# One product of each channel unit in two column parts, in a two-layer hybrid decoder trunk in float32

## The chip, the core and the metric

The kernel runs on one core of one Trainium2 chip. The metric is the device time of one execution in microseconds; lower is better.

## What is computed

The reference is a decoder trunk of two layers on an input of 256 tokens with 1024 features, all in float32. A layer is a half-step SwiGLU feed-forward network (FFN), a mixing block with two branches (a Mamba-2 state-space branch and a gated DeltaNet branch) on the same normalised input, and a second FFN:

```python
for l in range(DEPTH):                                   # DEPTH = 2, D_FF = 2816
    h = h + 0.5 * swiglu(rms_norm(h, ffn1_norm[l]), ffn1_w_in[l], ffn1_w_out[l])
    u = rms_norm(h, mix_norm[l])
    (z_s, xbc, dt_s, qkv, z_d, b_d, a_d, gate_s, gate_d) = jnp.split(u @ w_in[l], split_points, axis=-1)
    y_s = mamba2_branch(z_s, xbc, dt_s, ...)
    y_d = deltanet_branch(qkv, z_d, b_d, a_d, ...)
    merged = sigmoid(gate_s) * (y_s @ ssm_w_branch[l]) + sigmoid(gate_d) * (y_d @ dn_w_branch[l])
    h = h + merged @ w_out[l]
    h = h + 0.5 * swiglu(rms_norm(h, ffn2_norm[l]), ffn2_w_in[l], ffn2_w_out[l])
return rms_norm(h, final_norm)
```

The change touches the products of the normalised input with the first FFN matrix (`ffn1_w_in`, `ffn2_w_in`: all but their first 256 gate and up columns) and with those parts of `w_in` whose channels are needed on partitions: q, k, v and the output gate of the DeltaNet branch, and x, B and C of the Mamba branch.

## The kernel before

**Three products for one.** TensorE works on float32r, a rounded float32. To keep float32 accuracy each operand is split into a high half (its value rounded to float32r) and a low half (the rest), and a product is made as high x high + high x low + low x high, accumulated in PSUM. Each line of the kernel that issues a matmul issues one weight load with it; the profile shows both, as PE and PEld.

**Weights.** All large weights are streamed once, in an order fixed beforehand, in pieces of 128 x 1024. `load` (line 147) brings a piece by DMA into a `wraw` buffer (five of them), and `prep` splits it: ScalarE writes `whi` (line 67), VectorE writes `wlo` (line 70), into five buffers each. `take` hands the next split piece to a user and issues loads and splits ahead of it.

**Channel units.** The normalised input stands transposed in one tile `uW`, as eight k tiles of 128 features; each k tile has 256 token columns of the high half (`uTh`) and 256 of the low half (`uTl`). `chan_chunk` makes one channel unit: 256 output channels, in two halves `a` of 128, for all 256 tokens. It takes two weight pieces; for each half and each of the eight k tiles `mm3w` issues three matmuls whose stationary operand is a 128 x 128 block of weights and whose moving operand is 256 token columns: line 301 (high x high), line 302 (high weights x low input), line 303 (low weights x high input). A unit is so 2 x 8 x 3 = 48 matmuls into one PSUM bank. In the profile a unit goes by the name of its bank: `fc` in the FFNs, and `kk`, `qq`, `vv`, `zd`, `bc`, `xs` in the mixing block.

Each FFN has 20 such units and each mixing block 28 (four each of k, q, v, the output gate and B/C, eight of x), which makes 2 x (2 x 20 + 28) = 136 in all.

**What stands around them.** In an FFN a first unit in token layout (tile `f`, matmuls of 512 columns, lines 296 to 298) comes before the `fc` units. The first pair of `fc` units is broken by four transposes (`gT`, line 498). After groups of four or two `fc` units come block products with 512 columns (tile `p`), and at the end the closing products (tile `o`). Behind a unit, ScalarE and VectorE apply SiLU and the gate (FFN) or a short convolution of four taps (mixing block). In the mixing block the order of the units and of the small matmuls between them (triangular inverse, recurrence, decays) is written out by hand in `ORDER`; a scheduler puts every engine's instructions in order from priorities.

**Small matmuls.** Some matmuls of the mixing block are in plain float32: `psp` (line 635, 16 moving columns), `lb` (line 694, 32 columns), `cbb` (line 973, 256 columns). The profile records a plain float32 product as two matmuls.

Of the kernel before, what the change touches and what calls it, by code (L numbers as in the profile page):

```python
# [30 lines left out]
NSPL = 5  # L31
START = 2
PLACES = 6 * [40]

# [16 lines left out]
def trunk_kernel(ctx, tc, x, wst, wsm, norms, lpar, rpar, cst, out):  # L53
    nc = tc.nc
    V, A, G, PE = nc.vector, nc.scalar, nc.gpsimd, nc.tensor
# [121 lines left out]
    def ahead(key, n, fn):  # L177
        while state[key] < n:
            fn(state[key])
            state[key] += 1  # L180

    def take():
        j = state["taken"]
        state["taken"] = j + 1
        ahead("loaded", min(plan[min(j + NSPL, n_forms) - 1][2] + NRAW - 1, n_raw), load)
        ahead("prepped", min(j + 1 if state["hold"] else j + NSPL, n_forms), prep)
        return halves.pop(j)
# [44 lines left out]
    uT = uTh = uTl = None  # L232
    places = list(PLACES)

# [62 lines left out]
        PE.matmul(ps, lh, rl, start=False, stop=False)  # L297
        return PE.matmul(ps, ll, rh, start=False, stop=stop)  # L298

    def mm3w(ps, wh, wl, mh, ml, start, stop):  # L300
        PE.matmul(ps, wh, mh, start=start, stop=False)  # L301
        PE.matmul(ps, wh, ml, start=False, stop=False)  # L302
        PE.matmul(ps, wl, mh, start=False, stop=stop)  # L303

    def tok_chunk(ps, ks):

        ws = [(k, take()) for k in ks[::2]]
        for t in range(2):
            for k0, (wh, wl) in ws:
                for k in range(2):  # L310
# [8 lines left out]
                        kt == KT - 1,  # L319
                    )  # L320

    def chan_chunk(ps):

        ws = [take(), take()]
        for a in range(2):
            for q in range(2):
                wh, wl = ws[q]
                for k in range(4):
                    kt = 4 * q + k
                    c0 = k * 256 + a * P  # L330
                    mm3w(
                        ps[:, a * 256 : (a + 1) * 256],
                        wh[:, c0 : c0 + P],
                        wl[:, c0 : c0 + P],
                        uTh[:, kt, :],
                        uTl[:, kt, :],
                        kt == 0,
                        kt == KT - 1,
                    )

    def out_chunks(ps, stat, ks, last, group=1, split=False, first=None):
# [87 lines left out]
    def ffn(nxt):  # L429
# [55 lines left out]
        for c in range(FC - 1):  # L485
            g2 = tmp2("g2")
            for a in range(2):
                ps = accb("fc")
                chan_chunk(ps)
                sg = s2.tile([P, S], F32, tag="ca", name="sg", bufs=2)  # L490
                act(sg[:], ps[:, 0:S], AF.Silu)
                tt(g2[:, a * S : (a + 1) * S], sg[:], ps[:, S : 2 * S], ALU.mult)
                todo = todo[1:]
                if c == 0 and a == 0:
                    bank = trb("gT")
                    for k in range(2):
                        for t in range(2):
                            PE.transpose(bank[:, k * S + t * P : k * S + (t + 1) * P], gt[t][:, k * P : (k + 1) * P], ident)
                    split(0, bank[:].rearrange("p (k t) -> p k t", k=2))
            split(2 * c + 2, g2[:].rearrange("p (k t) -> p k t", k=2))  # L500
            if c + 1 <= PAIRS[-1][-1]:
                block_sums(c + 1, g2)
            if todo[0] == "A":
                if not pb:
                    pb.update({i: trb(f"p{i}") for i in (1, 6, 5, 7)})
                four = [
                    (pb[1], lambda p: stat(2 * p, 0), PAIRS[n]),
                    (pb[5], lambda p: sums(p, 0), PAIRS[n]),
                    (pb[7], lambda p: sums(p, 2), PAIRS[n]),
                    (pb[6], lambda p: sums(p, 1), PAIRS[n]),  # L510
                ]
                block_products(four, n == 0, n == len(PAIRS) - 1)
                todo = todo[1:]
                n += 1
# [5 lines left out]
    def mixer(l, nxt):  # L520
# [202 lines left out]
        def k_unit(hp):  # L723
            ps = accb("kk")
            chan_chunk(ps)
            for a in range(2):
                conv(ps[:, a * S : (a + 1) * S], 2 * hp + a, kP[:, hp, :, a, :], False)

            def rest():
                ktb, nb = turned(kP, hp)  # L730
                ts(kq[:, hp], nb[:], EPS, ALU.add)
                c1 = small([P, 4], "c1")
                V.reciprocal(out=c1[:], in_=kq[:, hp])
                tt(c1[:], c1[:], Bp[:, hp], ALU.mult)
                stt(c3n[:, hp], c1[:], -1.0, eG[:, hp], ALU.mult, ALU.mult)
                kkb = trb("kkb")
                own(kkb, kP, kP, hp)
                kk = s2.tile([P, 4, 64], F32, tag="s2", name="kk")
                for c in range(4):
                    act(kk[:, c], kkb[:, c * 64 : (c + 1) * 64], scale=c1[:, c : c + 1])  # L740
                for a in range(2):
                    rows_ = slice(64 * a, 64 * a + 64)
                    qev["ins"] = tt(Q[rows_, 4 * hp : 4 * hp + 4, rows_], dN[rows_, 4 * hp : 4 * hp + 4], kk[rows_], ALU.mult)
                for c in range(3):
                    act(kd[:, c, hp, :], ktb[:, c * P : (c + 1) * P], scale=dT[:, 4 * hp + c, 63:64])
                rsqrt(c2[:, hp], kq[:, hp], [P, 4])
                G.tensor_tensor(out=c2[:, hp], in0=c2[:, hp], in1=Bp[:, hp], op=ALU.mult)
                yield

            return rest()  # L750

        def q_unit(hp):
            ps = accb("qq")
            chan_chunk(ps)
            for a in range(2):
                conv(ps[:, a * S : (a + 1) * S], 8 + 2 * hp + a, qP[:, hp, :, a, :], False)

            def rest():
                _, nb = turned(qP, hp)
                ts(oe[:, hp], nb[:], EPS, ALU.add, EPS * 128.0, ALU.mult)  # L760
                qkb = trb("qkb")
                own(qkb, kP, qP, hp)
                for a in range(2):
                    rows_ = slice(64 * a, 64 * a + 64)
                    qk = qkb[rows_, 0:256].rearrange("p (c i) -> p c i", c=4)
                    tt(AT[rows_, 4 * hp : 4 * hp + 4, rows_], dT[rows_, 4 * hp : 4 * hp + 4], qk, ALU.mult)
                yield

            return rest()
# [589 lines left out]
```

## Time and profile before

| what | value |
|---|---|
| median of three runs | 1572.18 us (1570.56 to 1574.96) |
| the profiled execution | 1574.73 us |
| its span (first to last instruction) | 1573.0 us |
| granted TensorE clock | 0.999 |
| matmuls and weight loads recorded | 11432 each |
| high x high products of `fc` (line 301) | 1280, mean 281 ns |
| splitting a weight piece on VectorE (`wlo`, line 70) | 1222 ns each |
| splitting a weight piece on ScalarE (`whi`, line 67) | 1060 ns each |

In the profile a matmul's duration runs from its start to the end of its results; the next one starts long before that, so what a stream of matmuls costs is the step from start to start. "Idle before" is the time an engine had nothing to do ahead of a group of instructions.

### The profile page before, as it was taken

Reading aid. Unit: us, or ns where it says so; the run is one execution under the profiler, and the core shown is the slowest. Engines: PE = TensorE matmul, PEld = TensorE weight load, DVE = VectorE, ACT = ScalarE, POOL = GpSimd, SP = SyncE. Lnnn points to the kernel's source line nnn. Section 1 sums busy time; section 2 is a strip of 40 time slices with the busy share of each in tenths; the row PEclk is TensorE's granted clock in tenths of the full one; section 3 lists DMA queues with packets and bytes.
Section 4 is the critical chain, followed back from the end, with each engine's and each line's share of the span. In section 5 each row is a group of like instructions: output and inputs, shape, how many; then the busy total and the mean of one; then the engine's idle time right before and its main releaser. Section 6 shows DMA issues by size and latency. Waiting matters only on the chain.

```text
span 1573.0 us, 28904 instructions
## 1 busy us (share of the span) xinstructions
PE 1544.0 (98%) x11432; PEld 1393.4 (89%) x11432; DVE 1254.2 (80%) x1888; ACT 950.7 (60%) x1534; POOL 53.8 (3%) x60
## 2 busy tenths in 40 slices
PE   8999999999999999999999999999999999999997
PEld 7999779999888888999789997899998888899995
DVE  6878868967899766878777888699589987677887
ACT  5656568766666645555555566776756665455554
POOL 0000010000000000000000001010000000000000
PEclk9999999999999999999999999999999999999999
DMA  8565565553565566565765456555345556555554
GB/s 297 199 201 186 185 213 188 168 164 114 180 212 164 183 205 192 169 207 181 243 206 191 166 186 223 192 188 188 115 137 200 175 185 215 176 191 187 161 186 133
DMA packets 94221, 293.12 MB, mean 186 GB/s; under 512 B 22325, under 2 KB 23301, under 8 KB 93062
## 3 DMA queue, kind: packets, MB, share of 16 engines
q1 hardware_dynamic: 94086, 291.29, 56.5%
q8 instruction: 89, 1.46, 0.4%
q14 instruction: 46, 0.38, 0.1%
HBM read 289.33 MB, written 1.92 MB: 185 GB/s over the span
## 4 chain that ended last, share of the span: by engine, by line
PE 68%; DVE 14%; DMA 7%; issue 5%; ACT 4%; POOL 1%; SPq 0%; POOLq 0%; ACTq 0%; DVEq 0%
PE fc L301 9%; PE fc L302 9%; PE fc L303 9%; DVE wlo L70 7%; DMA wraw<-in_wst_dram 4%; PE b L298 3%; PE t L297 3%; PE t L296 2%; PE t L298 2%; PE b L297 2%; PE b L296 2%; DVE ca L73 2%; ACT whi L67 2%; PE p L297 2%; PE p L298 2%
## 5 line engine op out<-in xcount | busy, mean ns | idle before, releaser
L70 DVE TENSOR_TENSOR wlo<-wraw,whi 128x1024 fp32r<-128x1024 f32 x488 | 592.3, 1222 | 176.8 <-ACT whi L67 172.3
L67 ACT ACTIVATE whi<-wraw 128x1024 fp32r<-128x1024 f32 x488 | 511.9, 1060 | 276.9 <-PE fc L302 96.0
L301 PE MATMUL fc<-uW,whi 128*128 128x256 f32 x1280 | 359.2, 281 | 0.0
L303 PE MATMUL fc<-uW,wlo 128*128 128x256 f32 x1280 | 358.9, 280 | 0.0
L302 PE MATMUL fc<-uW,whi 128*128 128x256 f32 x1280 | 358.9, 280 | 0.0
L303 PEld LDWEIGHTS fc<-uW,wlo 128*128 128x128 f32 x1280 | 243.6, 190 | 0.0
L301 PEld LDWEIGHTS fc<-uW,whi 128*128 128x128 f32 x1280 | 241.7, 189 | 0.8
L302 PEld LDWEIGHTS fc<-uW,whi 128*128 128x128 f32 x1280 | 240.3, 188 | 0.8
L67 ACT ACTIVATE whi<-wfirst 128x1024 fp32r<-128x1024 f32 x64 | 68.0, 1062 | 65.9 <-PE fc L302 50.9
L296 PE MATMUL t<-whi,uW 128*128 128x512 f32 x256 | 102.1, 400 | 0.0
L297 PE MATMUL t<-wlo,uW 128*128 128x512 f32 x256 | 100.6, 393 | 0.4 <-DVE wlo L70 0.4
L298 PE MATMUL t<-whi,uW 128*128 128x512 f32 x256 | 100.7, 393 | 0.0
L70 DVE TENSOR_TENSOR wlo<-wfirst,whi 128x1024 fp32r<-128x1024 f32 x64 | 78.3, 1223 | 8.8 <-ACT whi L67 8.8
L296 PE MATMUL b<-whi,bh 128*128 128x512 f32 x192 | 76.3, 399 | 0.3 <-ACT bh L67 0.2
L297 PE MATMUL b<-wlo,bh 128*128 128x512 f32 x192 | 74.9, 390 | 0.0
L298 PE MATMUL b<-whi,bl 128*128 128x512 f32 x192 | 74.3, 394 | 0.6 <-DVE bl L70 0.6
L70 DVE TENSOR_TENSOR wfirst<-wraw,wfirst 128x1024 f32<-128x1024 f32 x48 | 58.7, 1222 | 19.1 <-DMA wraw<-in_wst_dram 18.7
L301 PE MATMUL xs<-uW,whi 128*128 128x256 f32 x256 | 72.7, 284 | 0.0
L297 PE MATMUL o<-wlo,gh 128*128 128x512 f32 x160 | 64.5, 403 | 7.1 <-DVE wlo L70 6.9
L303 PE MATMUL xs<-uW,wlo 128*128 128x256 f32 x256 | 71.1, 278 | 0.0
L302 PE MATMUL xs<-uW,whi 128*128 128x256 f32 x256 | 71.0, 277 | 0.0
L296 PE MATMUL o<-whi,gh 128*128 128x512 f32 x160 | 62.1, 392 | 0.3 <-ACT whi L67 0.3
(315 smaller groups left out, 3385.8 us busy)
## 6 DMA issues: line engine op xcount, KB each, us to landing
wraw<-in_wst_dram SPq DMA_DIRECT2D x504, 512.0 KB, 4.5
wfirst<-in_wst_dram SPq DMA_DIRECT2D x16, 512.0 KB, 6.1
dc<-rdram SPq DMA_DIRECT2D x8, 1024.0 KB, 8.5
nw<-in_norms_dram SPq DMA_DIRECT2D x6, 512.0 KB, 5.9
gb<-rdram SPq DMA_DIRECT2D x8, 256.0 KB, 5.5
h<-in_x_dram SPq DMA_DIRECT2D x4, 256.0 KB, 5.9
out_dram<-fo SPq DMA_DIRECT2D x4, 256.0 KB, 2.0
dq<-X SPq DMA_DIRECT2D x2, 256.0 KB, 5.4
```

The source lines that it names most:

```text
L67: return A.activation(out=o, in_=i, func=func, **kw)
L70: return V.tensor_tensor(out=o, in0=a, in1=b, op=op)
L73: return V.scalar_tensor_tensor(out=o, in0=a, scalar=s, in1=b, op0=op0, op1=op1)
L296: PE.matmul(ps, lh, rh, start=start, stop=False)
L297: PE.matmul(ps, lh, rl, start=False, stop=False)
L298: return PE.matmul(ps, ll, rh, start=False, stop=stop)
L301: PE.matmul(ps, wh, mh, start=start, stop=False)
L302: PE.matmul(ps, wh, ml, start=False, stop=False)
L303: PE.matmul(ps, wl, mh, start=False, stop=stop)
```

## The change

In half `a` = 0 of every channel unit, the high x low product of the second k tile (`kt` = 1) is issued as two matmuls with the same weights: one on the first `cut` token columns and one on the rest. `cut` follows a list of twelve widths from unit to unit, in the order in which the units are recorded; where it is 0 the product stays whole. All other products stay as they are, and the columns multiplied and the sums formed are the same.

```diff
+CUTS = [128, 64, 192, 32, 224, 16, 240, 96, 160, 48, 208, 0]
...
-    def mm3w(ps, wh, wl, mh, ml, start, stop):
+    def mm3w(ps, wh, wl, mh, ml, start, stop, cut=0):
         PE.matmul(ps, wh, mh, start=start, stop=False)
-        PE.matmul(ps, wh, ml, start=False, stop=False)
+        if cut:
+            PE.matmul(ps[:, :cut], wh, ml[:, :cut], start=False, stop=False)
+            PE.matmul(ps[:, cut:], wh, ml[:, cut:], start=False, stop=False)
+        else:
+            PE.matmul(ps, wh, ml, start=False, stop=False)
         PE.matmul(ps, wl, mh, start=False, stop=stop)
...
+    cuts = [CUTS[i % len(CUTS)] for i in range(140)]
+
     def chan_chunk(ps):
 
+        cut = cuts.pop(0)
         ws = [take(), take()]
...
                         kt == 0,
                         kt == KT - 1,
+                        cut if a == 0 and kt == 1 else 0,
                     )
```

## The prediction

> **What bounds the kernel now.** I read the page first, its busy times and its chain, then the matmul groups.
>
> ```profile
> PE 1544.0 (98%) x11432; PEld 1393.4 (89%) x11432; DVE 1254.2 (80%) x1888; ACT 950.7 (60%) x1534; POOL 53.8 (3%) x60
> ...
> PE 68%; DVE 14%; DMA 7%; issue 5%; ACT 4%; POOL 1%; SPq 0%; POOLq 0%; ACTq 0%; DVEq 0%
> ...
> L301 PE MATMUL fc<-uW,whi 128*128 128x256 f32 x1280 | 359.2, 281 | 0.0
> L303 PE MATMUL fc<-uW,wlo 128*128 128x256 f32 x1280 | 358.9, 280 | 0.0
> L302 PE MATMUL fc<-uW,whi 128*128 128x256 f32 x1280 | 358.9, 280 | 0.0
> ```
>
> PE is busy for 98% of the span and carries 68% of the chain. The last column is the idle time before a group: 0.0 us in the three products of a channel unit. So the change works where PE runs matmul behind matmul, and PE time added there is path time. PE does wait, elsewhere:
>
> ```profile
> PE o L297 <- DVE wlo L70: 6.9, 15, 0.9
> PE hnT L262 <- DVE hn L73: 6.2, 7, 1.0
> ```
>
> These follow from the last matmul before them and do not shrink when channel units get longer, so nothing gives the added time back.
>
> A matmul of 281 ns does not cost 281 ns, since matmuls overlap. Its cost is the step from start to start, read from the timeline (start, duration, engine, line), first and last row of two unbroken runs:
>
> ```profile
> 76.09 0.28 PE L301 MATMUL fc<-uW,whi 128*128 128x256 f32 x1
> 98.58 0.28 PE L303 MATMUL fc<-uW,wlo 128*128 128x256 f32 x1
> ```
>
> ```profile
> 237.19 0.28 PE L302 MATMUL kk<-uW,whi 128*128 128x256 f32 x1
> 264.17 0.28 PE L303 MATMUL kk<-uW,wlo 128*128 128x256 f32 x1
> ```
>
> The first run is four units, 191 steps: 22.49 / 191 = 117.8 ns. The second is five units less one matmul, 238 steps: 26.98 / 238 = 113.4 ns. Same shapes, same granted clock, two steps 4.4 ns apart. It is not the tile: windows of 20 us (length, PE busy, count, clock) over fc runs alone show both, 172 or 173 matmuls or 179.
>
> ```profile
> 33.00:53.00 20.00, 20.00 (x172) 1.00 0.81 284
> 820.00:840.00 20.00, 20.00 (x179) 1.00 0.59 187
> 856.00:876.00 20.00, 20.00 (x173) 1.00 0.54 181
> ```
>
> A run keeps its step until something breaks the row of matmuls. The four transposes gT of an FFN's first block are such a break, and it turned the step over both ways:
>
> ```profile
> 30.59 0.60 PE L498 MATMUL gT<-cs,sg 128*128 128x128 f32 x4
> ...
> 809.74 0.60 PE L498 MATMUL gT<-cs,sg 128*128 128x128 f32 x4
> ```
>
> ```profile
> 25.80:30.50 4.70, 4.70 (x44) 1.00 0.89 288
> 31.40:36.10 4.70, 4.70 (x43) 1.00 0.91 332
> 804.80:809.50 4.70, 4.70 (x43) 1.00 0.86 293
> 810.80:815.50 4.70, 4.70 (x44) 1.00 0.72 236
> ```
>
> So the change has two terms: the price of one more matmul in a unit, and what the break that it makes does to the step of the some 45 matmuls behind it.
>
> **Part by part.** The change adds 125 matmuls: 136 channel units (20 in each of four FFNs, 28 in each of two mixers), of which every twelfth, 11 in all, has width 0. Each added one brings its own weight load, as every matmul here does (11432 of both). Columns multiplied stay the same.
>
> *Term A, the pieces.* No row shows an fp32r matmul under 256 columns. The nearest narrow row with full 128x128 weights is psp, fp32, 16 columns; its weight loads:
>
> ```profile
> 235.96 0.96 PE L635 MATMUL psp<-dq,cs 128*128 128x16 f32 x8
> ```
>
> ```profile
> 236.41 0.41 PEld L635 LDWEIGHTS psp<-dq,cs 128*128 128x128 f32 x3
> 236.74 0.19 PEld L694 LDWEIGHTS lb<-ac,cs 128*128 128x128 f32 x1
> ```
>
> Three loads from 236.41, the next at 236.74: 0.33 / 3 = 110 ns a step, at a sixteenth of the columns of the 113 ns step. With almost nothing to stream, the load sets the step. So two pieces cost about 2 x 112 = 224 ns whatever the cut, where one whole product costs 116.3 ns (the mean of the two steps by the shares below): 107.7 ns more, times 125 = 13.5 us. Bounds: two steps at 110 give 104 ns and 13.0 us; two at 117.8 give 119 ns and 14.9 us.
>
> From below, 512 columns:
>
> ```profile
> 99.38 0.39 PE L296 MATMUL p<-whi,gh 128*128 128x512 f32 x1
> 100.97 0.39 PE L297 MATMUL p<-wlo,bsb 128*128 128x512 f32 x1
> ```
>
> Seven steps: 1.59 / 7 = 227 ns, exactly twice 113.4. By these two widths alone a matmul has no fixed price, and the pieces would cost nothing. I take the narrow row, since it is the only one on the pieces' side of 256.
>
> The Trainium skill, "TensorE: Matmul & The Clock Gate", section "Back-to-back issue gap", gives a stream of load-and-matmul pairs at 128 columns as about 81 ns a matmul; by that, an estimate, the pair costs 162 ns and term A about 6 us. Psp's 110 ns speaks against it here.
>
> *Term B, the step behind the break.* A matmul at the short step lasts 276 ns, at the long one 281, so a group's mean gives its share of long steps:
>
> ```profile
> L302 PE MATMUL xs<-uW,whi 128*128 128x256 f32 x256 | 71.0, 277 | 0.0
> L302 PE MATMUL bc<-uW,whi 128*128 128x256 f32 x128 | 36.5, 286 | 0.0
> L302 PE MATMUL vv<-uW,whi 128*128 128x256 f32 x128 | 35.8, 280 | 0.0
> L302 PE MATMUL zd<-uW,whi 128*128 128x256 f32 x128 | 35.7, 279 | 0.0
> L302 PE MATMUL qq<-uW,whi 128*128 128x256 f32 x128 | 35.3, 276 | 0.0
> L302 PE MATMUL kk<-uW,whi 128*128 128x256 f32 x128 | 35.3, 276 | 0.0
> ```
>
> With fc's 358.9 / 1280 = 280.4: fc 0.88, vv 0.74, zd 0.58, xs 0.27, kk and qq 0; bc, blurred by waits, I set at 0.6. Weighted: 0.66 of 6528 matmuls are long. One whole share is 6528 x 4.4 ns = 29 us. The cut resets the step in 125 units, so afterwards the share is that of outcomes of such breaks. Between gT's flips both ways and the narrow psp, which left the short step behind it, I take a half: (0.50 - 0.66) x 29 = -4.6 us. Ends: share 0, -19 us; share 1, +10 us.
>
> *What moves.* In the built program POOL's order stays. On DVE and ACT some weight splits change places with neighbours. In SP's queue of each layer one weight load goes behind the transfers dq, T and TT of the inverse, and T waits there for dq, in the chain of waits:
>
> ```profile
> 319.34 5.91 DMA dq<-X
> ```
>
> A channel unit (48 steps, 5.6 us) takes two pieces, and five raw and five split buffers stand ahead of PE, over 20 us: I put this at 0. Were the cover gone, it would cost up to that 5.9 us a layer, or at a swapped split one
>
> ```profile
> L70 DVE TENSOR_TENSOR wlo<-wraw,whi 128x1024 fp32r<-128x1024 f32 x488 | 592.3, 1222 | 176.8 <-ACT whi L67 172.3
> ```
>
> that is 1.2 us. No wait is added: the pieces read the tiles of the product before them.
>
> *Sum.* 13.5 - 4.6 = +8.9 us on the profiled execution's 1574.73 (span 1573.0 and 1.7 around it): 1583.6. That execution lies 2.55 us above the median of the runs, so against 1572.18 I forecast 1581.
>
> **The rivals.** *All breaks fall short* (the other side): every cut leaves the short step, in the fc units above all, where nine tenths are long. -19.2 + 13.5 = -5.7 us: 1566.5. It is a gain as soon as the share left long is under 0.66 - 13.5/29 = 0.19. For it: psp. Against it: gT at 30.59, which left the long step.
>
> *All breaks fall long*, as after every p block quoted here: +9.9 + 13.5 = +23.4: 1595.6. Against it: the same.
>
> *Loads hide.* The two 512 and 256 steps hold below 256 too; A is 0, and with B 1567.6, without B 1572.2. Psp speaks against it. This is the direction of the skill's 81 ns.
>
> *Narrow fp32r streams slower.* Then width matters. An fp32 row at 256 columns against the same at fp32r:
>
> ```profile
> L973 PE MATMUL cbb<-BC x16: 379/380/483, 411.7 to 1191.0; 128*128 128x256 f32 x16
> L302 PE MATMUL kk<-uW,whi x128: 276/276/283, 237.2 to 1040.4; 128*128 128x256 f32 x128
> ```
>
> 104 ns more over 256 columns, so 0.84 ns a column in place of 0.44. Each piece then takes the larger of 111 ns and 0.84 x width: 55 ns more per pair, averaged over the eleven widths, and 6.9 us more: 1588. With fp32's two records a product (1.68 ns a column) it is 240 ns a pair and 30 us more: 1611. The skill's "FP8 and Floating Point Precision", section "TensorE Precision Notes", has true FP32 at four passes, which would be that upper end. Nothing in the trace shows it or excludes it for fp32r.
>
> That the change doesn't do what it says is excluded: the built program holds 125 more matmuls.
>
> **How the numbers follow.** Forecast 0.62, all short 0.10, all long 0.14, loads hide 0.06, narrow slower 0.08. The forecast's own range, shares 0.30 to 0.75 long, is 13.5 - 10.4 to 13.5 + 2.6: 1575 to 1588. All short (0.10) is left out below, and of narrow slower the upper half and the worst of all long above: 1571 to 1597 for 8 in 10. 0.3% is 4.7 us, about what a measurement of this kernel can tell from no change: faster means under 1567.5, slower over 1576.9. Faster: most of all short, 0.08. Same: most of loads hide, the rest of all short, and the forecast's low edge, 0.20. Slower: 0.72.
>
> **What would show it.** In the profile after: fc's groups with some 70 to 80 pieces; steps of about 112 ns at both pieces of every width, 240 as well as 16 (term A); if the 240 piece steps at 200 ns, the last rival holds. Fc means nearer 278 than 280, and kk and qq above 276 (term B). Idle time before the channel groups still 0. I am wrong if the pieces step under 60 ns, or if one width always leaves the short step and the others never do, so that the share is not near a half.

## The result and the profile after

The changed kernel takes 1596.8 us (median of 4 runs, 1593.08 to 1597.42) where the kernel before takes 1572.38 us beside it: a ratio of 1.0149, 95% interval 1.0128 to 1.0170. That is 24.4 us slower, where 8.8 were forecast. The profiled execution took 1596.97 us with a span of 1595.1 us, 22.1 us longer than that of before.

The page of the changed kernel, its busy times, its chain and its `fc` groups (busy, mean ns, idle time before):

```profile
PE 1551.0 (97%) x11557; PEld 1399.2 (88%) x11557; DVE 1255.8 (79%) x1888; ACT 949.1 (60%) x1534; POOL 50.0 (3%) x60
...
PE 62%; DVE 17%; DMA 7%; issue 6%; ACT 5%; SPq 1%; POOL 1%; POOLq 0%; ACTq 0%; DVEq 0%
...
L308 PE MATMUL fc<-uW,wlo 128*128 128x256 f32 x1280 | 358.0, 280 | 0.0
L302 PE MATMUL fc<-uW,whi 128*128 128x256 f32 x1280 | 354.7, 277 | 0.0
L307 PE MATMUL fc<-uW,whi 128*128 128x256 f32 x1206 | 333.6, 277 | 0.0
```

Two things stand here that the forecast did not have. The `fc` means on lines 302 and 307 are 277 ns, below the forecast's "nearer 278 than 280": most of these matmuls are at the short step. (Line 308 stays at 280 because the matmul behind a narrow piece is recorded as longer, as the timeline below shows.) And of the 22.1 us only 7.0 are added PE busy time (1551.0 against 1544.0). The other 15.1 us are idle PE: span less busy time was 29.0 us and is 44.1. The chain agrees: PE carries 62% instead of 68%, and DVE 17% instead of 14%.

What PE waited for after the change (us in total, times, longest):

```profile
PE o L298 <- DVE wlo L71: 10.3, 21, 0.9
PE cbb L982 <- DVE vb L71: 5.7, 2, 3.3
...
PE yT L1106 <- DVE og L74: 3.1, 2, 1.5
PE b L297 <- ACT bh L68: 2.6, 2, 1.3
```

The waits for `vb`, `og` and `bh` belong to the mixing blocks. The one for `vb` was 1.3 us before; those for `og` and `bh` do not come to 0.3 us in that view of before. Measured between the same matmuls in each trace, from a mixing block's first `t` to the next FFN's first `f`, the stages came out as follows (us):

| stage | before | after | all cuts, old order (below) |
|---|---|---|---|
| mixing block, layer 0 | 408.5 | 417.6 | 410.3 |
| mixing block, layer 1 | 407.4 | 421.7 | 410.6 |
| four FFNs together | 740.0 | 739.0 | 737.2 |

So the FFNs, which hold 74 of the 125 cuts, became no longer, and the two mixing blocks carry the whole loss: 23.4 us.

**One wait followed back.** Layer 1 of the changed kernel: the issue of the transfer for `dc` (the decays), VectorE's timeline and the matmul that waits (start, duration, and in brackets the idle time before and what ended it):

```profile
1193.22 0.91 SPq L998 DMA_DIRECT2D dc<-rdram  x2
1203.76 2.29 DVE L71 TENSOR_TENSOR dc<-dc,ac 128x2048 f32<-128x2048 f32 x1 [4.61 <-DMA dc<-rdram]
1205.97 0.68 DVE L71 TENSOR_TENSOR vb<-ob,os 128x512 f32<-128x512 f32 x1
1206.71 1.22 PE L982 MATMUL cbb<-BC 128*128 128x256 f32 x2 [3.32 <-DVE vb L71]
```

The same place before:

```profile
1179.70 0.91 SPq L989 DMA_DIRECT2D dc<-rdram  x2
1187.72 2.29 DVE L70 TENSOR_TENSOR dc<-dc,ac 128x2048 f32<-128x2048 f32 x1 [0.68 <-DMA dc<-rdram]
```

In both kernels `vb` stands behind `dc` on VectorE, and `dc` waits for a transfer. Before, VectorE had 0.68 us to wait; now it has 4.61 us, and PE has nothing left to run while `vb` is late. Most of this is the transfer's own time: from its first issue to the start of `dc` it is 10.5 us here and was 8.0 us before, 2.5 us more, and PE's wait grew by 2.8 us (3.32 against 0.51). Nor does it clearly go with the order of issue: at this place PE waits 1.9 us in the run below with all cuts and the old order, and 1.1 us in the one with the new order and no cut. Why the transfer took longer was not followed up.

The wait then costs a second time. Windows of 2 us over that place after the change (length, busy times, and, third from the end, the granted clock), and the same place before:

```profile
1206.00:1208.00 2.00, 1.29 (x4) 1.11 (x5) 2.00 (x4) 0.80 (x2) 0.00 (x0) 0.50 0.03 12
1208.00:1210.00 2.00, 2.00 (x7) 1.61 (x7) 1.78 (x6) 0.74 (x3) 0.80 (x1) 0.50 0.42 115
```

```profile
1190.00:1192.00 2.00, 1.50 (x8) 1.20 (x8) 1.96 (x6) 0.97 (x3) 0.00 (x0) 1.00 0.74 303
```

PE is busy again, but at half its clock. In windows of 2 us over the whole span, the changed kernel has three such stretches inside the mixing blocks (416 to 422, 1204 to 1214, 1266 to 1272 us). The missing share of the clock, summed, is 6.8 us. The kernel before has no stretch below full clock there.

**Another.** The tile `oT` and who waits for its reader `og`, before and after:

```profile
L73 DVE SCALAR_TENSOR_TENSOR og<-oT,lp,zdT x8: 740/748/752, 467.2 to 1255.6; 128x512 f32<-128x512 f32 x8
...
  ACT bh L67: 1.0, 4
```

```profile
L74 DVE SCALAR_TENSOR_TENSOR og<-oT,lp,zdT x8: 742/743/750, 474.1 to 1275.9; 128x512 f32<-128x512 f32 x8
...
  ACT bh L68: 10.1, 4
...
  PE yT L1106: 3.1, 2
```

`oT` came 4.3 us later after the change (465.8 against 461.5), `og` 6.9 us later (474.1 against 467.2): it now stands behind more of VectorE's other work. ScalarE's `bh` waits 10.1 us instead of 1.0, and PE's `yT` waits, which it did not. VectorE around this `og`, before and after:

```profile
467.18 0.74 DVE L73 SCALAR_TENSOR_TENSOR og<-oT,lp,zdT 128x512 f32<-128x512 f32 x1
...
468.29 1.22 DVE L70 TENSOR_TENSOR wlo<-wraw,whi 128x1024 fp32r<-128x1024 f32 x1
```

```profile
472.53 1.21 DVE L71 TENSOR_TENSOR wlo<-wraw,whi 128x1024 fp32r<-128x1024 f32 x1
...
474.12 0.74 DVE L74 SCALAR_TENSOR_TENSOR og<-oT,lp,zdT 128x512 f32<-128x512 f32 x1
```

A weight split that came behind `og` now comes ahead of it. This one is the order of issue.

### The profile page after: what moved, and what is told of

It is laid out like the page before. It is cut to its first block, busy times and chain, and to the rows that moved or that the text cites. A ratio compares the mean times of both kernels' runs of the same rounds, so it can differ in the third digit from the quotient of the medians.

```text
span 1595.1 us, 29147 instructions
## 1 busy us (share of the span) xinstructions
PE 1551.0 (97%) x11557; PEld 1399.2 (88%) x11557; DVE 1255.8 (79%) x1888; ACT 949.1 (60%) x1534; POOL 50.0 (3%) x60
## 4 chain that ended last, share of the span: by engine, by line
PE 62%; DVE 17%; DMA 7%; issue 6%; ACT 5%; SPq 1%; POOL 1%; POOLq 0%; ACTq 0%; DVEq 0%
PE fc L308 8%; PE fc L302 8%; DVE wlo L71 8%; PE fc L307 8%; DMA wraw<-in_wst_dram 4%; DVE ca L74 3%; PE b L297 3%; PE b L298 3%; PE b L299 3%; PE t L299 3%; PE t L298 3%; PE t L297 3%; ACT whi L68 2%; PE xs L308 2%; PE xs L302 2%
## 5 line engine op out<-in xcount | busy, mean ns | idle before, releaser
L302 PE MATMUL fc<-uW,whi 128*128 128x256 f32 x1280 | 354.7, 277 | 0.0
L307 PE MATMUL fc<-uW,whi 128*128 128x256 f32 x1206 | 333.6, 277 | 0.0
L302 PEld LDWEIGHTS fc<-uW,whi 128*128 128x128 f32 x1280 | 240.8, 188 | 0.8
L307 PEld LDWEIGHTS fc<-uW,whi 128*128 128x128 f32 x1206 | 226.4, 188 | 0.8
L302 PE MATMUL xs<-uW,whi 128*128 128x256 f32 x256 | 73.0, 285 | 0.0
L307 PE MATMUL xs<-uW,whi 128*128 128x256 f32 x241 | 67.1, 278 | 0.0
```

## The experiments

The first question was which of two things costs the time: the cut itself (its pieces and the step behind it), or the order of issue, which the added matmuls change in the built program. To part them, the order of issue of TensorE, VectorE, ScalarE and SyncE was written out as a table, and each instruction tied behind its predecessor. The tie sets an order and adds no wait. The table with the old order and no cut was not run, so what the table does by itself is not shown. "Old order" is the order of the kernel before, "new order" that of the changed kernel.

```diff
+PIN = {"PE": "0+10 18+17 10+4 35 ...", "DVE": "...", "Activation": "...", "SP": "..."}
+    for a, b in zip(line, line[1:]):          # line: one engine's instructions in that order
+        tc.add_manual_dep(b, a.name, mybir.DependencyInfo(mybir.DependencyClass.NoSync, ...))
```

**All cuts, old order** (`e1_cuts_old_order`). The changed kernel with that table; each second piece stands directly behind its first.

> All 125 cuts as in the changed kernel, but every engine issues in the order of the kernel before (each second part right behind its first). Theory ORDER (of the 24.4 us that were lost, the pieces and the step behind them make up some 3 to 6 us in the channel units, and the rest comes from the order of issue, which the extra matmuls made the scheduler change in the mixing blocks): 1575 to 1579 us. Rival PIECES (the pieces themselves delay what the mixing blocks wait for, whatever the order): 1592 us or more.

Measured: 1575.35 us, 1.0002 of before (0.9993 to 1.0011), inside the range that was expected if the order costs the time. All 125 cuts together cost nothing that can be measured. By the table of stages the mixing blocks, where more of the steps were short already, are 5.0 us longer than before, and the FFNs 2.8 us shorter. The page, PE's wait for `vb`, and the wait of `bh` for `og`:

```profile
PE 1544.5 (98%) x11557; PEld 1392.8 (88%) x11557; DVE 1253.7 (80%) x1888; ACT 950.1 (60%) x1534; POOL 53.7 (3%) x60
```

```profile
PE cbb L1141 <- DVE vb L230: 3.3, 2, 1.9
```

```profile
  ACT bh L227: 1.0, 4
```

PE is busy for 0.5 us more than before with 125 more matmuls, `bh` waits 1.0 us again, and no stretch at half clock is left in the mixing blocks. The wait for `vb` stays at 3.3 us with the old order. The changed kernel's span is 20.5 us longer than this one's (1595.1 against 1574.6). Of that, 14.0 us are idle PE (44.1 against 30.1), and 6.5 us are PE busy time (1551.0 against 1544.5), close to the 6.8 us of missing clock.

**No cut, whole new order** (`e2_whole_new_order`). The kernel before with the changed kernel's table, less the second pieces.

> No cut at all, but every engine issues in the order of the changed kernel. Theory ORDER: 1587 to 1593 us, with the waits of cbb, oT, yT and o as in the changed kernel. Rival PIECES: 1570 to 1575 us, as before.

Measured: 1592.36 us, 1.0111 (1.0097 to 1.0125), 17.4 us over before on that chip. What PE waited for:

```profile
PE yb L974 <- DMA TT<-dq: 5.4, 2, 3.1
...
PE yT L1252 <- DVE og L228: 3.5, 2, 1.9
...
PE b L451 <- ACT bh L222: 2.6, 2, 1.3
```

The waits for `og` and `bh` are those of the changed kernel, without a single cut. So the order is a cause by itself.

The 17.4 us hide a gain. In this trace PE is idle for 15.5 us more than before (44.5 against 29.0) and 8.5 us of clock are missing in the mixing blocks, 24 us together, but the span is only 17.8 us longer (1590.8 against 1573.0). The difference of some 6 us is the step: counted from start to start, the share of long steps is 0.45 here and 0.66 before, without a cut, and 0.21 of the forecast's 29 us is 6 us. The share lies between 0.45 and 0.51 in all five runs with a table and no cut, also in the two whose FFNs have the old order. In the FFNs it is the units two to eight, behind `gT`, that turned: they were long in three of four FFNs before and are long in one of the twenty in these five runs. Whether the table does this or chance is open; two traces of the changed kernel also differ from each other in which units are long.

**The changed kernel again** (`e7_changed_again`), on the chip of the two runs that follow.

> The changed kernel itself on the chip of e5 and e6. If the loss is the order alone (pieces and short steps cancel, as e1 showed), it stands as far over before as e5 and e6 together, or up to 6 us more where the cuts take away time in which a wait was hidden: 17 to 25 us over before.

Measured: 1593.76 us, 1.0122 (1.0102 to 1.0141). Cuts alone (1.0002) and order alone (1.0111) multiply to 1.0113, inside that interval, so the totals need nothing else, though the terms beneath them do not simply add: the new order alone had 8.5 us of missing clock and more long steps. The first comparison gave 1.0149; the two intervals overlap. This trace has 3.4 us of missing clock in the mixing blocks where the first had 6.8; that difference would be most of the 4.3 us between the two profiled executions (1592.64 and 1596.97).

**The new order in one part of the mixing blocks.** The kernel before with the new order only up to the B/C units and with them, that is units, inverse and recurrence (`e5_new_order_first_part`), or only behind them, that is decays, Mamba units and branch products (`e6_new_order_second_part`).

> No cut. The order of issue of the kernel before, except in the first part of each mixing block (from the q, k and v units through the inverse and the recurrence), which has the order of the changed kernel: there the units of B and C stand elsewhere among the small matmuls, and one weight load goes behind the transfers dq, T and TT. Theory ORDER, with the added time where PE waits in e2 (bc 7.5, cbb 2.9, yb 0.8 us longer there): 9 to 12 us over before. Rival: the order matters in the second part alone: within 2 us of before.

> No cut. The order of issue of the kernel before, except in the second part of each mixing block (decays, Mamba units, branch products), which has the order of the changed kernel: there the transposes oT and yT and the VectorE work behind them stand later. Theory ORDER, with the added time in e2 (oT 3.9, yT 3.1, b 2.3, xs 1.9 us longer there): 8 to 11 us over before. Rival: the order matters in the first part alone: within 2 us of before. With e5 it should add up to the some 17 us of e2, or to 24 us if e2's fc units had the short step more often by luck alone.

Measured: 1582.87 us, 1.0048 (1.0033 to 1.0064), and 1584.64 us, 1.0058 (1.0040 to 1.0076). The first part came out a little under what was expected, the second inside. Together they make 1.0106, beside 1.0111 for the whole. What PE waited for, first part and then second:

```profile
PE yb L977 <- DMA TT<-dq: 5.3, 2, 3.8
```

```profile
PE cbb L1128 <- DVE vb L225: 3.6, 2, 2.4
PE yT L1252 <- DVE og L228: 3.5, 2, 1.9
PE b L451 <- ACT bh L222: 2.6, 2, 1.3
```

Each part brings its own waits: `TT` in the first, `og` and `bh` in the second. Each trace has 5.1 us of missing clock. In the second all of it lies in the mixing blocks; in the first 1.7 us of it lies in an FFN (at 950 us), behind a wait of 1.8 us for `wlo`.

**Which engine's order.** No cut, and the new order on all engines but one: SyncE's load queue in the old order (`e9_new_order_old_load_queue`), or TensorE in the old order (`e10_old_order_on_tensor_engine`).

> No cut; TensorE, VectorE and ScalarE issue in the order of the changed kernel, SyncE's queue in that of the kernel before. Theory 'late results': the new order costs by the waits it makes on TensorE and by the stretches at a granted clock of 0.50 behind them. With the whole new order TensorE waited 5.4 us for TT behind dq, twice, and the clock lay at a half for about 3.4 us behind each wait, half of which is lost (3.4 us in all). With SyncE's old order that weight load stands ahead of dq again; if the wait came from there, both go: 5.4 + 3.4 = about 9 us less than the whole new order, some 8 to 9 us (0.5 to 0.6%) over the kernel before. Rival 'TensorE's own order': the small matmuls stand where nothing covers them, whatever the loads do, and the time stays at that of the whole new order, 17 us over.

> No cut; TensorE issues in the order of the kernel before, VectorE, ScalarE and SyncE in that of the changed kernel. Theory 'late results': VectorE makes og behind the large decay products and vb behind the transfer dc, whatever TensorE does in the meantime, so the waits for og, bh and vb stay and grow, because TensorE asks for them at the old, earlier places: at least the 17 us of the whole new order, and up to 30. Rival 'TensorE's own order': with TensorE's old order the cover is back and the time is within 5 us of the kernel before.

Measured: 1599.5 us, 1.0167 (1.0148 to 1.0185), and 1596.91 us, 1.0148 (1.0134 to 1.0162). With the old load queue both expectations missed: it got slower than with the whole new order, not faster. PE's wait, and SyncE's first issue of `T`, with the old queue and then with the new (the run without a cut above):

```profile
PE yb L974 <- DMA TT<-dq: 10.6, 2, 6.2
```

```profile
324.56 0.33 SPq L968 DMA_DIRECT2D T<-dq  x1
```

```profile
321.80 0.33 SPq L968 DMA_DIRECT2D T<-dq  x1
```

In these two traces, putting the weight load behind `dq` and `T` lets `T` start 2.8 us earlier. It is not what makes PE wait for `TT`; it takes half of that wait away.

With TensorE's old order the time is 23.2 us over before, inside the 17 to 30 us of the theory of late results, so the rival, that TensorE's own order is at fault, falls:

```profile
PE yT L1255 <- DVE og L231: 5.7, 2, 2.9
...
PE xs L459 <- ACT whi L225: 5.2, 2, 2.6
```

PE comes to `yT` as early as before and waits longer for the late `og` (5.7 us against 3.5), and a channel unit `xs` now waits for its weight split. The wait for `TT` is not in its list any more, so that one was TensorE asking earlier; yet the sum is higher without TensorE's new order than with it. By these ratios, taken on different chips (1.0148 and 1.0167 against 1.0111), TensorE's and SyncE's new orders each gain beside the new order of the others. That leaves the order on VectorE and ScalarE as what costs, by elimination: it was not run alone, nor were the two tried one at a time, so it stays open which of their moves costs most.

**Two cuts a unit, old order** (`e3_two_cuts_old_order`), for the price of a cut where the step is short already.

```diff
-                        cut if a == 0 and kt == 1 else 0,
+                        cut if a == 0 and kt in (1, 5) else 0,
```

> As e1, with a second cut of the same width in the sixth k tile of the same half: 125 more pieces, same order of issue. By the price that the trace of the changed kernel shows behind a cut (113 to 140 ns beyond a whole product, steps behind it included): 14 to 17 us over e1. By the narrow row alone (two steps of 112 ns in place of one of 116, my term A): 13.5 us over e1. If a second piece were hidden by the load of the next weights: under 5 us over e1.

Measured: 1587.29 us, 1.0080 (1.0068 to 1.0093), 11.9 us over one cut a unit on the same chip, less than the 13.5 us and the 14 to 17 us expected.

```profile
PE 1557.0 (98%) x11682; PEld 1407.1 (89%) x11682; DVE 1253.8 (79%) x1888; ACT 951.8 (60%) x1534; POOL 53.6 (3%) x60
```

PE is busy for 12.5 us more than with one cut, 100 ns for each of the 125 second cuts. That is near the forecast's 107.7 ns, and no second gain comes with it: a short step cannot be made short again.

**Few cuts, old order** (`e4_few_cuts_old_order`, `e8_fewer_cuts_old_order`). If the gain comes from leaving the long step and the price is paid by every cut, one cut behind each break should have most of the gain at a fifth of the price. 28 cuts of width 96, then 26 at slightly moved places, since in two FFNs of the first the long step went on for seven units:

```diff
+        ffn_cuts = [96 if i in (0, 1, 8, 12, 16, 18) else 0 for i in range(20)]   # then (1, 2, 8, 12, 16, 18)
+        cuts += ffn_cuts + [96 if n in ("v1", "v2") else 0 for n in ORDER if n in UNITS] + ffn_cuts   # then "v2" alone
```

> Only 28 cuts, all of width 96: in the units 0, 1, 8, 12, 16 and 18 of each FFN (the first behind each block of 512 columns, and the one that gT breaks) and in v1 and v2 of each mixing block; order of issue of the kernel before. If a cut turns the long step into the short one and the step then holds until the next break: long share of fc under 0.15, 28 x 0.127 = 3.6 us paid and some 14 us won: 1560 to 1563 us. Rival: the short step in the changed kernel has another cause, or has to be renewed in every unit: 1571 to 1577 us.

> As e4 with 26 cuts of width 96: in each FFN the units 1, 2, 8, 12, 16, 18 (the second unit behind gT is cut too, since in two FFNs the cut right behind gT left the long step for seven units; unit 0 is whole), in each mixing block v2 alone. Won against e4: two FFN stretches of six units at 0.21 us each, 2.6 us, and two cuts of 0.13 us; lost: unit 0 at the long step, 0.2 us in each FFN less the cut. 9.5 to 11 us under before. If the second cut fails there too: 8 us under before, as e4.

Measured: 1566.70 us, 0.9949 (0.9936 to 0.9963), and 1567.45 us, 0.9952 (0.9936 to 0.9968). Both beat both kernels, by 8.3 and 7.1 us under before on their chips; both fell short of what was expected. Windows of 20 us over `fc` runs, the first kernel and then the second (length, PE busy and count, and so on):

```profile
33.00:53.00 20.00, 20.00 (x172) 20.00 (x171) 13.93 (x24) 10.10 (x16) 0.00 (x0) 1.00 0.84 293
820.00:840.00 20.00, 20.00 (x173) 20.00 (x172) 14.10 (x23) 10.22 (x14) 0.00 (x0) 1.00 0.56 182
```

```profile
33.00:53.00 20.00, 20.00 (x179) 20.00 (x178) 14.41 (x25) 10.58 (x18) 0.00 (x0) 1.00 0.85 302
820.00:840.00 20.00, 20.00 (x179) 20.00 (x178) 14.78 (x23) 10.88 (x15) 0.00 (x0) 1.00 0.56 174
```

The second kernel has the short step in both windows where the first has the long one, yet the two times cannot be told apart. Its PE is busy 10.0 us less than before in the trace, and its time 7.1 us less. The rest is idle PE, 2.7 us more than before (31.7 against 29.0); why it waits more is not settled.

The cuts need not have won all of this. The last twelve units of an FFN are long in every FFN of the six traces without a cut and short in every FFN of the second kernel: 4 x 12 x 48 x 4.4 ns = 10.1 us, less 26 cuts at the 127 ns worked out below, 3.3 us, is 6.8 us. That part is the cuts'. The units two to eight are mostly short in the runs with a table and no cut too, so a gain there is not shown to be theirs.

## Why the prediction was wrong, point by point

**"What moves … I put this at 0"** is the step that failed. The forecast looked at weight splits and at one weight load in SyncE's queue, found cover of over 20 us for them, and put the rest of the changed order at nothing. It did not look at the order of the small work in the mixing blocks, where `og` follows other work on VectorE, `bh` follows `og` on ScalarE, and PE stands behind both and behind `TT`. The new order, without a cut, costs 17.4 us: in its trace 15.5 us more of idle PE and 8.5 us of missing clock, less some 6 us by shorter steps. The upper bound given there was also read off the wrong thing: the load queue's move is worth a gain with this order, and the half clock behind a wait was in no bound.

**Term A, the pieces,** held in kind. The timeline of the changed kernel at a cut of 16 and at one of 240 columns (start, duration):

```profile
53.27 0.28 PE L302 MATMUL fc<-uW,whi 128*128 128x256 f32 x1
53.38 0.17 PE L304 MATMUL fc<-uW,whi 128*128 128x16 f32 x1
53.41 0.36 PE L305 MATMUL fc<-uW,whi 128*128 128x240 f32 x1
53.61 0.28 PE L308 MATMUL fc<-uW,wlo 128*128 128x256 f32 x1
53.73 0.28 PE L302 MATMUL fc<-uW,whi 128*128 128x256 f32 x1
...
58.83 0.28 PE L302 MATMUL fc<-uW,whi 128*128 128x256 f32 x1
58.94 0.27 PE L304 MATMUL fc<-uW,whi 128*128 128x240 f32 x1
59.05 0.18 PE L305 MATMUL fc<-uW,whi 128*128 128x16 f32 x1
59.08 0.36 PE L308 MATMUL fc<-uW,wlo 128*128 128x256 f32 x1
59.28 0.28 PE L302 MATMUL fc<-uW,whi 128*128 128x256 f32 x1
```

The narrow piece steps 0.03 us, under the 60 ns that the forecast named as its own refutation. But the matmul behind it steps 0.20 us, in either order of the two. From one high x high product to the next it takes 0.46 and 0.45 us, where three whole steps of 113.4 ns are 0.34: the price is 0.11 to 0.12 us at both widths. So the sum was near and its picture (about 112 ns for each piece) was not: the missing time appears one matmul later. Over all widths, in the run with all cuts and the old order, the matmuls up to where the step is even again cost 127 ns more a cut on average, 15.9 us in place of 13.5. The price is the same from 16 to 240 columns, so it does not depend on how the columns are divided; whether the added weight load or the added matmul sets it was not tried apart. By the 81 ns a matmul of the Trainium skill, "TensorE: Matmul & The Clock Gate", section "Back-to-back issue gap", it would be about 6 us, an estimate; the trace does not bear that out for these products.

**Term B, the step behind the break,** had the right sign and a third of its size. Counted step by step, the share of long steps among the channel units' matmuls fell from 0.66 to 0.13 with all cuts in the old order, not to 0.5. By the forecast's own 29 us for a whole share that is -15.4 us in place of -4.6. In that trace 118 of the 125 cuts have the short step behind them: the break that psp made was its nearest relative, not gT or the p blocks. With 15.9 for term A the sum is +0.5 us, and +0.4 was measured. How much of the -15.4 us is the cuts' own is not shown in full: 10.1 us of it are the last twelve units of the FFNs, and some 6 us of short steps came in the runs with a table and no cut as well.

**The rivals.** *Loads hide* and *narrow fp32r streams slower* fall by the rows above: the price is there, and no piece of 240 columns steps at 200 ns by itself, only behind a narrow one. *All breaks fall short* was nearly the truth for the step. Its condition, a share under 0.19, was met, but term A was larger than it reckoned, so the gain came to nothing until most of the cuts were taken out. The total of *all breaks fall long*, 1595.6, is nearest to the measured one, but by luck: the share of long steps in the changed kernel is 0.18, not 1.

**"Nothing gives the added time back"** did not hold fully. Between one cut a unit and two, PE's wait `o <- wlo` went from 6.7 to 5.1 us and that for `vb` from 3.3 to 2.6: that fits a slower PE coming later to work that is late by itself.

## What to carry to other kernels

An edit that adds instructions on one engine can move what stands on the others; compare the order of issue on every engine, and above all that of the small dependent work, before costing the edit alone. To part the two, write the old order out by hand and put the edit into it: here that showed 0.4 us where the whole edit cost 24. Where a matmul stream holds one of two steps, one break at the right place may be a gain, and the same break everywhere pays its price each time.

## What the runs showed of the hardware

A short wait of PE can cost more than itself. The changed kernel's timeline, layer 0 (two places) and layer 1:

```profile
417.47 1.22 PE L982 MATMUL cbb<-BC 128*128 128x256 f32 x2 [2.38 <-DVE vb L71]
...
476.93 0.50 PE L297 MATMUL b<-whi,bh 128*128 128x512 f32 x1 [1.29 <-ACT bh L68]
...
1267.55 0.79 PE L297 MATMUL b<-whi,bh 128*128 128x512 f32 x1 [1.29 <-ACT bh L68]
```

Behind the 2.38 us the clock lay at a half. The other two rows are the same place in two layers with the same wait, each behind another of 1.5 us; in the first the clock held, in the second it fell, and the matmul took 0.79 us in place of 0.50. The stretches cost 1.7 or 3.4 us each, which is 3.4 or 6.8 us at half clock. The Trainium skill, "TensorE: Matmul & The Clock Gate", section "What's actually happening", has the clock follow a free-running window of about 3.4 us; the lengths, and that the same wait does and does not trip it, agree with that. Its advice in "Why this matters for your kernels", to avoid idle gaps over some 3 us, is too lenient here: 2.38 us was enough.

The two steps of one and the same matmul, 113.4 and 117.8 ns, hold for some 200 matmuls in the runs quoted, and a cut, whatever its width, leaves the short one behind it in about nine cases of ten (118 of 125, and 110 of 124 in the changed kernel's trace). What sets the two steps was not tried and stays open.
